# Modulation rounds with a ring and fixed steps of their own beside the blocks of w2, half by half on TensorE or on VectorE, and w2 loaded two blocks to a buffer

## The chip, the cores and the metric

The kernel runs on one core of a Trainium2 chip. The metric is the device time of one execution in microseconds (us). The engines named below are TensorE (PE, with its weight loads as PEld), VectorE (DVE), ScalarE (ACT), GpSimd (POOL) and SyncE (SP), which issues the loads.

## What is computed

A trunk of two layers over 256 latent tokens and 256 context tokens of width 1024. Each layer is a feed-forward half-step, a mixer (even: spatial gating and attention; odd: mLSTM) and a second feed-forward half-step. Every half-step and mixer takes its shift, scale and gate from the modulation, nine vectors of 1024 for each layer, once for the latent and once for the context tokens. All is float32.

```python
def modulate(z, g, shift, scale):
    return rmsnorm(z, g) * (1 + scale) + shift

def swiglu(z, w13, w2):
    gate, up = jnp.split(z @ w13, 2, axis=-1)
    return (jax.nn.silu(gate) * up) @ w2

s_lat = jax.nn.silu(c)
s_ctx = jax.nn.silu(c_ctx)[None, :]
for l in range(DEPTH):
    m_l = (s_lat @ mod_w[l] + mod_b[l]).reshape(b, N_MOD, 1, d)
    m_c = (s_ctx @ mod_w[l] + mod_b[l]).reshape(1, N_MOD, 1, d)
    h = h + 0.5 * m_l[:, 2] * swiglu(modulate(h, norm_g[l, 0], m_l[:, 0], m_l[:, 1]), ffn_w13[l, 0], ffn_w2[l, 0])
    ...
    h = h + m_l[:, 5] * y_l
    h = h + 0.5 * m_l[:, 8] * swiglu(modulate(h, norm_g[l, 2], m_l[:, 6], m_l[:, 7]), ffn_w13[l, 1], ffn_w2[l, 1])
    ...
```

## The kernel before

**Products.** A float32 weight is split into two parts of reduced float32, `whi` (ScalarE's cast, in `wsplit`) and `wlo` (VectorE's subtraction of that from the raw weight), and activations likewise; each product is three matmuls, high by high, high by low and low by high (`mm3`, L116 to L118). The split weights lie in a ring of four (`NWH`), so splits run up to four blocks ahead of PE. Raw weights lie in a ring of four buffers of 1 MB, `rawp`.

**Stages.** In time: a start; the first ffn of layer 0 to 410.7 us; the even mixer to 550; the second ffn of layer 0 to 968.6; the first ffn of layer 1 to 1346.5; the odd mixer to about 1545; the last ffn, latent tokens only. The first three are `ffn512`, both sets of tokens together, 512 columns. It cuts the hidden width of 22 tiles of 128 into two chunks, 12 and 10 (`CHUNKS`). For a chunk it first makes the hidden columns, pair by pair, from w13 (seven products of 24 matmuls of 256 columns for a pair, L791), then multiplies them by w2: four blocks of output columns (`dp`, two PSUM banks each), each over the chunk's tiles in blocks of up to four (three blocks in the first chunk; 4, 4 and 2 in the second). A whole block is 24 matmuls of 512 columns. A block of w2 is 512 KB and takes a whole buffer of `rawp`. In the second chunk the last `dp` is done in two halves of 256 columns, and the next norm's sums stand beside it. After a `dp`, `finish` adds the result to the residual with the gate. The gate of a half-step is itself modulation, needed in the first chunk: there the first `dp`'s `finish` is kept back in `late` until after the first block of the second `dp`, the fourth in all.

**Modulation.** The 9 x 1024 columns of `mod_w` of a layer are 18 rounds of 512 columns; a round's weights are two loads of 1 MB, its halves. Four rounds are done at the start in another form. The others:

- On VectorE (`mod_round_dve`, 24 rounds): eight tiles of 128 rows, for each set of tokens one multiply-add over 128 x 512 (L265 the first, L267 the rest), 16 operations, or 8 where only latent tokens need the round (from `LATROUND`). Four small matmuls then add VectorE's 128 partial sums into a PSUM bank (`mod_ps`, L277). When a group of rounds (`GROUPS`) is full, it is copied out, transposed and written to `modT`.
- On PE (`mod_direct`, 8 rounds in pairs): 16 matmuls a pair, which the trace records as 32, of 32 stationary columns into one bank (`mdir_ps`, L311); then `direct_columns`: a copy on ScalarE (L324), four transposes (`mdirT_ps`) and two small operations on VectorE. One pair stands in the first ffn and one in the third, between the first and the second `dp` of the first chunk; two pairs in the even mixer.

**Order.** Engines run their instructions in program order, as a scheduler lays it out from the order of the code and from priorities. `tick` calls `fill` after each block of w2; `FILL` gives 2.6 steps of VectorE rounds per block in the first chunk and 2.2 in the second, each raised by `LEAD`; the small matmuls are raised by `GROUPED`. All rounds take their loads from `rawp`, by `wraw` (L99), in the one SyncE queue that also issues w2 (L961). The odd mixer's `run` calls `fill` too, but in the profile no round is left for it.

Of the kernel before, what the change touches and what calls it, by code (L numbers as in the profile page):

```python
# [26 lines left out]
LEAD = 60  # L27
GROUPED = 400
FILL = ((2.6, 2.2), (2.6, 2.2), (2.6, 2.2))
GROUPS = (((6, 12), (16, 18)), ((0, 4), (6, 10), (10, 12), (12, 16), (16, 18)))  # L30
LATROUND = (1, 10)
MIXDIRECT = {4: (12, 13), 8: (14, 15)}
SOFF = 2
FILLODD = range(13, 25)
# [12 lines left out]
def tile_trunk(  # L47
# [132 lines left out]
    s_st = const.tile([P, KD, SOFF + 32], F32, name="s_st")  # L180
    dve.memset(s_st, 0.0)
# [39 lines left out]
    def mod_round(k, raw):  # L221

        ps = abank("mod_ps")
        for i in range(4):
            for j in range(4):
# [3 lines left out]
                    s_st[:, kh * 4 + i, SOFF:],  # L229
# [18 lines left out]
    filler = []  # L248
    group = {}
    current = [None]  # L250
    turn = [None]
    hidp = [None]
    until = [(1, 17)]

    def mod_round_dve(l, r, hp):

        nv = 1 if (l, r) >= LATROUND else 2
        acc = hp.tile([P, nv, 512], F32, tag="mod_acc", name="mod_acc", bufs=1)
        for kh in range(2):
            raw = wraw(mod_w[l], 4 * kh, 4, r * 512, 512)  # L260
            for k in range(4):
                for v in range(nv):
                    s1 = s_st[:, 4 * kh + k, SOFF + v : SOFF + v + 1]
                    if kh == 0 and k == 0:
                        dve.tensor_scalar(acc[:, v], raw[:, k], s1, None, op0=ALU.mult)  # L265
                    else:
                        dve.scalar_tensor_tensor(acc[:, v], raw[:, k], s1, acc[:, v], op0=ALU.mult, op1=ALU.add)  # L267
                    if nv == 2 and v == 1 or nv == 1 and k % 2 == 1:
                        yield
        r0, n = next((a, b - a) for a, b in GROUPS[l] if a <= r < b)  # L270
        m = r - r0
# [3 lines left out]
        with tc.high_priority(offset=GROUPED):  # L275
            for j in range(4):
                pe.matmul(  # L277
                    ps[32 * j : 32 * (j + 1), : nv * P],
                    onehot[:, MAXG - 1 - m : MAXG + 31 - m],
                    acc[:, :, j * P : (j + 1) * P],  # L280
                    start=(m == 0),
                    stop=(m == n - 1),
                    tile_position=(0, 32 * j),
                )
        if m < n - 1:
            return

        sb = tmp.tile([P, T], F32, tag="sil", name="mod_sb2", bufs=NSIL)
        act.copy(sb[:, : nv * P], ps[:, : nv * P])
        pt = abank("modT_ps")  # L290
# [3 lines left out]
        for v in range(nv):  # L294
# [5 lines left out]
            )  # L300

    def mod_direct(l, rounds):
# [3 lines left out]
        for m, r in enumerate(rounds):  # L306
            raws = [wraw(mod_w[l], 4 * kh, 4, r * 512, 512) for kh in range(2)]
            for i in range(2):
                for j in range(4):
                    k = 2 * j + i  # L310
                    pe.matmul(  # L311
                        ps[32 * j : 32 * (j + 1), :],
                        s_st[:, k, SOFF - 2 * m : SOFF + 32 - 2 * m],
                        raws[k // 4][:, k % 4],
                        start=(m == 0 and i == 0),
                        stop=(m == n - 1 and i == 1),
                        tile_position=(0, 32 * j),
                    )
        return lambda: direct_columns(l, rounds, ps)

    def direct_columns(l, rounds, ps):
        n = len(rounds)
        sb = tmp.tile([P, T], F32, tag="sil", name="mdir_sb", bufs=NSIL)
        act.copy(sb, ps)  # L324
        pt = abank("mdirT_ps")
        for b in range(4):
            tr(pt[:, b * P : (b + 1) * P], sb[:, b * P : (b + 1) * P])
        red = tmp.tile([P, 4, 4], F32, tag="mod_red", name="mod_red", bufs=1)
        dve.tensor_reduce(
            red, pt.rearrange("p (b j c) -> p b c j", b=4, j=4)[:, :, :4], axis=AX.X, op=ALU.add  # L330
# [7 lines left out]
        )  # L338

    def fill(n=1, more=True):  # L340

        for _ in range(n):
            while True:
                if current[0] is None:
                    if not filler or filler[0] > until[0]:
                        return
# [11 lines left out]
    def mvec(l, v):  # L358
# [3 lines left out]
        while current[0] is not None or filler:  # L362
            nxt_round = turn[0] if current[0] is not None else filler[0]
            if nxt_round > (l, end):
                break
# [1587 lines left out]
```

## Time and profile before

| | us |
|---|---|
| median of three runs (1728.83 to 1732.63) | 1730.41 |
| profiled execution, its own time | 1736.36 |
| its span in the trace | 1734.6 |
| PE busy in the span | 1677.1 (97%) |
| DVE busy | 1328.6 (77%) |
| ACT busy | 769.8 (44%) |

The profile is of one execution, so its durations add up against 1736.36, not against the median. Busy time of PE counts overlapping matmuls once; a 512-column matmul is recorded with 0.39 us but the next starts 0.23 us later, so starts, not durations, give PE's pace. The granted clock is a share of 2.4 GHz; over the span it is 0.985.

### The profile page before, as it was taken

Reading aid. Unit: us, or ns where it says so; the run is one execution under the profiler, and the core shown is the slowest. Engines: PE = TensorE matmul, PEld = TensorE weight load, DVE = VectorE, ACT = ScalarE, POOL = GpSimd, SP = SyncE. Lnnn points to the kernel's source line nnn. Section 1 sums busy time; section 2 is a strip of 40 time slices with the busy share of each in tenths; the row PEclk is TensorE's granted clock in tenths of the full one; section 3 lists DMA queues with packets and bytes.
Section 4 is the critical chain, followed back from the end, with each engine's and each line's share of the span. In section 5 each row is a group of like instructions: output and inputs, shape, how many; then the busy total and the mean of one; then the engine's idle time right before and its main releaser. Section 6 shows DMA issues by size and latency. Waiting matters only on the chain.

```text
span 1734.6 us, 29987 instructions
## 1 busy us (share of the span) xinstructions
PE 1677.1 (97%) x12310; PEld 1520.0 (88%) x12310; DVE 1328.6 (77%) x2138; ACT 769.8 (44%) x1217; POOL 89.6 (5%) x109
## 2 busy tenths in 40 slices
PE   7999899999999999989999999999999999999998
PEld 5799589978977999968997999769998799899998
DVE  5897688876765699998888898689886955695554
ACT  4454125523665465412552555214542654364443
POOL 0000000002442000000000000000000001100000
PEclk8999999999999999999999999999999999999999
DMA  9445543253235033465325333575256432136552
GB/s 277 139 137 186 201 158 122 93 177 119 84 136 146 29 119 102 154 213 164 120 83 184 96 128 110 210 264 169 86 195 185 133 111 73 50 128 213 189 179 71
DMA packets 227868, 248.54 MB, mean 143 GB/s; under 512 B 10648, under 2 KB 193940, under 8 KB 227732
## 3 DMA queue, kind: packets, MB, share of 16 engines
q1 hardware_dynamic: 227700, 246.63, 44.6%
q8 instruction: 96, 1.57, 0.4%
q14 instruction: 40, 0.33, 0.1%
q10 hardware_dynamic: 32, 0.01, 0.0%
HBM read 245.56 MB, written 1.05 MB: 142 GB/s over the span
## 4 chain that ended last, share of the span: by engine, by line
PE 55%; issue 12%; DVE 9%; DMA 2%; ACT 1%; POOL 1%; DVEq 0%; SPq 0%; POOLq 0%; ACTq 0%
PE pb L791 11%; PE ps L118 8%; PE ps L116 8%; PE ps L117 8%; PE pc L791 5%; PE pa L791 2%; DVE mod_acc L267 2%; DVE wlo L111 2%; PE ps L1045 2%; PE ps L1046 2%; PE ps L1047 2%; DMA raw<-in_mod_w_dram 1%; PE nd_ps L1744 1%; PE nd_ps L1741 1%; PE sc_ps L1336 1%
## 5 line engine op out<-in xcount | busy, mean ns | idle before, releaser
L110 ACT CAST whi<-raw 128x1024 fp32r<-128x1024 f32 (+2 forms) x204 | 206.9, 1017 | 369.5 <-PE ps L117 169.4
L111 DVE TENSOR_TENSOR wlo<-raw,whi 128x1024 fp32r<-128x1024 f32 (+2 forms) x204 | 239.6, 1181 | 108.4 <-ACT whi L110 108.0
L116 PE MATMUL ps<-hh,whi 128*128 128x512 f32 (+1 forms) x764 | 273.4, 358 | 10.1 <-ACT whi L110 10.1
L118 PE MATMUL ps<-hh,wlo 128*128 128x512 f32 (+1 forms) x764 | 271.3, 356 | 3.2 <-DVE wlo L111 3.2
L117 PE MATMUL ps<-hl,whi 128*128 128x512 f32 (+1 forms) x764 | 271.3, 355 | 0.0
L116 PE MATMUL ps<-zhi,whi 128*128 128x256 f32 (+2 forms) x688 | 209.1, 307 | 3.5 <-ACT zhi L416 1.8
L118 PE MATMUL ps<-zhi,wlo 128*128 128x256 f32 (+2 forms) x688 | 207.6, 305 | 1.8 <-DVE wlo L111 1.7
L117 PE MATMUL ps<-zlo,whi 128*128 128x256 f32 (+2 forms) x688 | 208.0, 304 | 0.0
L267 DVE SCALAR_TENSOR_TENSOR mod_acc<-raw,s_st,mod_acc 128x512 f32<-128x512 f32 x280 | 196.3, 746 | 11.1 <-DMA raw<-in_mod_w_dram 10.0
L110 ACT CAST whi<-rpl 128x1024 fp32r<-128x1024 f32 x116 | 121.7, 1052 | 149.1 <-DMA rpl<-in_ffn_w_dram 41.1
L116 PEld LDWEIGHTS ps<-hh,whi 128*128 128x128 f32 x764 | 145.9, 191 | 34.6 <-ACT whi L110 11.4
L118 PEld LDWEIGHTS ps<-hh,wlo 128*128 128x128 f32 x764 | 146.1, 191 | 30.0 <-DVE wlo L111 4.8
L117 PEld LDWEIGHTS ps<-hl,whi 128*128 128x128 f32 x764 | 145.9, 191 | 22.2 <-issue 1.2
L111 DVE TENSOR_TENSOR wlo<-rpl,whi 128x1024 fp32r<-128x1024 f32 x116 | 140.7, 1220 | 15.2 <-ACT whi L110 14.9
L116 PEld LDWEIGHTS ps<-zhi,whi 128*128 128x128 f32 x688 | 131.2, 191 | 11.5 <-ACT zhi L416 2.3
L118 PEld LDWEIGHTS ps<-zhi,wlo 128*128 128x128 f32 x688 | 130.9, 191 | 7.7 <-DVE wlo L111 2.4
L117 PEld LDWEIGHTS ps<-zlo,whi 128*128 128x128 f32 x688 | 131.3, 191 | 4.8 <-issue 0.4
L791 PE MATMUL pc<-zhi,wlo 128*128 128x256 f32 x440 | 124.1, 282 | 0.0
L791 PE MATMUL pc<-zlo,whi 128*128 128x256 f32 x440 | 123.9, 282 | 0.0
L791 PE MATMUL pc<-zhi,whi 128*128 128x256 f32 x440 | 123.8, 281 | 0.0
L791 PEld LDWEIGHTS pc<-zhi,wlo 128*128 128x128 f32 x440 | 83.2, 189 | 0.0
L791 PEld LDWEIGHTS pc<-zhi,whi 128*128 128x128 f32 x440 | 83.2, 189 | 0.0
(383 smaller groups left out, 4223.6 us busy)
## 6 DMA issues: line engine op xcount, KB each, us to landing
raw<-in_mod_w_dram SPq DMA_DIRECT2D x64, 1024.0 KB
raw<-in_ffn_w_dram SPq DMA_DIRECT2D x62, 512.0 KB
raw<-in_ffn_w_dram SPq DMA_DIRECT2D x30, 1024.0 KB
rpl<-in_ffn_w_dram SPq DMA_DIRECT2D x58, 512.0 KB
rsum<-in_ffn_w_dram SPq DMA_DIRECT2D x29, 512.0 KB
ra<-in_ffn_w_dram SPq DMA_DIRECT2D x29, 512.0 KB
raw<-in_ml_w_in_dram SPq DMA_DIRECT2D x12, 1024.0 KB
mod<-in_mod_w_dram SPq DMA_DIRECT2D x16, 512.0 KB
```

What stands on the lines that cost most here:

```text
L110: act.copy(hi, view)
L111: dve.tensor_tensor(lo, view, hi.bitcast(F32), op=ALU.subtract)
L116: pe.matmul(ps, ah, bh, start=start, stop=False)
L117: pe.matmul(ps, ah, bl, start=False, stop=False)
L118: pe.matmul(ps, al, bh, start=False, stop=stop)
L267: dve.scalar_tensor_tensor(acc[:, v], raw[:, k], s1, acc[:, v], op0=ALU.mult, op1=ALU.add)
L791: pe.matmul(o, a[:, k, cs], b[:, k], start=fresh and j == 0 and k == 0 and n == 0, stop=j == 1 and k == 3 and n == 2, skip_group_check=True,)
L1045: pe.matmul(o, zh, wh[:, k % 4], start=(k == 0), stop=False)
L1046: pe.matmul(o, zh, wl[:, k % 4], start=False, stop=False)
L1047: pe.matmul(o, zl, wh[:, k % 4], start=False, stop=(k == KD - 1))
L1336: pe.matmul(sc[:, :nk], qst[t][:, p, w], kst[:, w, part, key0 * P : key0 * P + nk], start=(part == 0), stop=(part == 1),)
L1741: pe.matmul(nd3[:, d, :], wts[h][:, d * HT + t * P : d * HT + (t + 1) * P], vs[p][:, t, w, :], start=True, stop=False)
```

## The change

1. *A ring for modulation.* Inside `ffn512`, loads of modulation go to a ring `q` of two buffers of 1 MB (shared with one w13 block and two saved products of a pair), by `mod_load`. In the mixers they stay in `rawp`, with a priority of their own (`RAWLEAD`); the last ffn has one buffer for them. The stationary columns lie closer together for it (`s_flat`).
2. *Two blocks of w2 to a buffer*: `load_block` hands out halves of a 1 MB buffer.
3. *Fixed steps.* `STEPS` names, for each block of w2 in order, what is put behind it: D is the next step of `mod_direct`, which is half a round on PE (four instructions, eight records), or the transposes; V is one tile of a VectorE round, two operations, or the end of a round. `FILL`, `fill` and `tick` go, and so does the priority.
4. *Who does which round.* `DIRECT` gives each `ffn512` a pair and a single round on PE, `ONDVE` three rounds on VectorE. The even mixer gets a third pair (`MIXDIRECT`); the odd mixer gets one pair and four VectorE rounds (12 to 15, latent tokens only); the last ffn gets rounds 16 and 17 on VectorE. In all 17 rounds are on PE and 15 on VectorE.
5. *The gate* and the kept `finish` come once the round is there (`made`): after the fifth block instead of the fourth.
6. *Small matmuls* of a VectorE round: one set of four for each set of tokens, half as wide (L298), without priority in `ffn512`.

```diff
-FILL = ((2.6, 2.2), (2.6, 2.2), (2.6, 2.2))
...
+DIRECT = (((0, (4, 5)), (0, (9,))), ((0, (16, 17)), (1, (3,))), ((1, (4, 5)), (1, (9,))))
+ONDVE = (((0, 6), (0, 7), (0, 8)), ((1, 0), (1, 1), (1, 2)), ((1, 6), (1, 7), (1, 8)))
+STEPS = (
+    ("D", "D", "D", "DV", "DVV", "VV", "VV", "V", "VVV", "VV", "VV", "VV", "V"),
+    ("V", "V", "V", "VV", "V", "VD", "V", "VD", "VD"),
+)
-MIXDIRECT = {4: (12, 13), 8: (14, 15)}
+MIXDIRECT = {1: (10, 11), 4: (12, 13), 7: (14, 15)}
+ODDDIRECT = (10, 14, 18)
...
-FILLODD = range(13, 25)
+FILLODD = range(9, 33)
...
+    def mod_load(l, r, kh):
+
+        if mraw[0] is None:
+            with tc.high_priority(offset=RAWLEAD):
+                return wraw(mod_w[l], 4 * kh, 4, r * 512, 512)
+        raw = mraw[0]().rearrange("p (k c) -> p k c", c=512)
+        nc.sync.dma_start(
...
-    def mod_direct(l, rounds):
+    def mod_direct(l, rounds, halves=1):
 
         n = len(rounds)
         ps = abank("mdir_ps")
         for m, r in enumerate(rounds):
-            raws = [wraw(mod_w[l], 4 * kh, 4, r * 512, 512) for kh in range(2)]
-            for i in range(2):
+            for kh in range(2):
+                raw = mod_load(l, r, kh)
                 for j in range(4):
...
+                if (halves == 2 or kh == 1) and (m < n - 1 or kh == 0):
+                    yield
         sb = tmp.tile([P, T], F32, tag="sil", name="mdir_sb", bufs=NSIL)
         act.copy(sb, ps)
+        yield
...
+            mraw[0] = lambda: hp.tile([P, 2048], F32, tag="q", name="mraw", bufs=2)
...
                     def load_block(k0, n):
-                        r = rawp.tile([P, 2048], F32, tag="raw", name="raw2", bufs=4)[:, : n * 256]
-                        v = r.rearrange("p (k c) -> p k c", c=256)
+                        if not spare:
+                            t = rawp.tile([P, 2048], F32, tag="raw", name="raw2", bufs=4)
+                            spare.extend([half_tile(t, 1), half_tile(t, 0)])
+                        v = spare.pop()[:, :n]
...
-                            if ch == 0 and dp == 1 and k0 == 0:
-                                if len(late) > 1:
-                                    late.pop(0)()
+                            if half == 0:
+                                advance(next(todo, ""))
+                            if late and made(l, 2 + 6 * i):
                                 dve.tensor_scalar(gate, mvec(l, 2 + 6 * i), 0.5, None, op0=ALU.mult)
-                                late.pop(0)()
-                            if not last:
-                                tick(rates[ch] * n / 4)
...
+        work = (s for r in range(12, 16) for s in mod_round_dve(l, r))
+        direct = mod_direct(l, (10, 11))
...
                 if ran[0] in FILLODD:
-                    fill(1)
+                    with tc.high_priority(offset=LEAD):
+                        next(work, None)
+                if ran[0] in ODDDIRECT:
+                    next(direct, None)
```

PE in the w2 stage of the first ffn, first chunk, before: the end of the third block, the whole pair (16 instructions) with its transposes and one set of sums, then the fourth block.

```order
962 L117 MATMUL ps<-hl,whi 128x512
963 L118 MATMUL ps<-hh,wlo 128x512
964 L311 MATMUL mdir_ps<-raw,s_st 32x512 x16
965 L121 MATMUL mdirT_ps<-ident,mdir_sb 128x128
966 L277 MATMUL mod_ps<-mod_acc,onehot 32x256 x4
967 L121 MATMUL mdirT_ps<-ident,mdir_sb 128x128 x3
968 L116 MATMUL ps<-hh,whi 128x512
969 L117 MATMUL ps<-hl,whi 128x512
```

PE in the same stage after the change: the end of the first block, one half-round (four instructions, from the ring's buffer `mraw`), the start of the second block. The same row stands behind the second, third and fourth block, 25 rows apart.

```order
939 L125 MATMUL ps<-hl,whi 128x512
940 L126 MATMUL ps<-hh,wlo 128x512
941 L336 MATMUL mdir_ps<-mraw,s_st 32x512 x4
942 L124 MATMUL ps<-hh,whi 128x512
943 L125 MATMUL ps<-hl,whi 128x512
```

The pair has come apart into four pieces, the first of them two blocks earlier, and its transposes no longer follow it at once.

SyncE's loads around the same stage before: modulation (L99) and w2 (L961) take turns in the one ring, and each w2 row is one block.

```order
53 L961 DMA raw_1833<-in_ffn_w_dram 128x4x256
54 L99 DMA raw<-in_mod_w_dram 128x4x512 x4
55 L961 DMA raw_1894<-in_ffn_w_dram 128x4x256
56 L99 DMA raw<-in_mod_w_dram 128x4x512
57 L961 DMA raw_1953<-in_ffn_w_dram 128x4x256
58 L99 DMA raw<-in_mod_w_dram 128x4x512
59 L961 DMA raw_1991<-in_ffn_w_dram 128x4x256
60 L961 DMA raw_2031<-in_ffn_w_dram 128x4x256
```

SyncE's loads there after the change: w2 blocks 3 to 10 (L971) stand together, with one modulation load (L269) between, and the other loads of the pair's halves follow the w13 sum `rsum`.

```order
47 L971 DMA raw_1822<-in_ffn_w_dram 128x4x256 x2
48 L971 DMA raw_1903<-in_ffn_w_dram 128x4x256
49 L269 DMA mraw<-in_mod_w_dram 128x4x512
50 L971 DMA raw_1903<-in_ffn_w_dram 128x4x256
51 L971 DMA raw_1991<-in_ffn_w_dram 128x4x256 x2
52 L971 DMA raw_2056<-in_ffn_w_dram 128x4x256 x2
53 L772 DMA rsum<-in_ffn_w_dram 128x4x256
54 L269 DMA mraw<-in_mod_w_dram 128x4x512 x3
```

Modulation's loads have moved behind w2's, and four of them no longer stand in one piece ahead of a block.

VectorE in the odd mixer, in the chain of scans that makes the gates, before:

```order
1296 L1540 SCALAR_TENSOR_TENSOR M<-LI,mst 64x128
1297 L1545 TENSOR_TENSOR mst<-bcum,M 64x1
1298 L1540 SCALAR_TENSOR_TENSOR M<-LI,mst 64x128
1299 L1545 TENSOR_TENSOR mst<-bcum,M 64x1
1300 L1540 SCALAR_TENSOR_TENSOR M<-LI,mst 64x128
1301 L111 TENSOR_TENSOR wlo<-raw,whi 128x1024
1302 L1545 TENSOR_TENSOR mst<-bcum,M 64x1
```

The same chain after the change:

```order
1198 L287 TENSOR_SCALAR mod_acc<-raw,s_st 128x512
1199 L1551 SCALAR_TENSOR_TENSOR M<-LI,mst 64x128
1200 L289 SCALAR_TENSOR_TENSOR mod_acc<-raw,s_st,mod_acc 128x512
1201 L1556 TENSOR_TENSOR mst<-bcum,M 64x1
1202 L119 TENSOR_TENSOR wlo<-raw,whi 128x1024
1203 L1551 SCALAR_TENSOR_TENSOR M<-LI,mst 64x128
1204 L289 SCALAR_TENSOR_TENSOR mod_acc<-raw,s_st,mod_acc 128x512
1205 L1556 TENSOR_TENSOR mst<-bcum,M 64x1
1206 L289 SCALAR_TENSOR_TENSOR mod_acc<-raw,s_st,mod_acc 128x512
```

Four modulation operations stand between the scans now, and further on one more split stands among the copies ahead of the convolution.

## Rows read from the trace of the kernel before

**Rows 1.** The page's busy times: us, share of the span, instructions.

```profile
PE 1677.1 (97%) x12310; PEld 1520.0 (88%) x12310; DVE 1328.6 (77%) x2138; ACT 769.8 (44%) x1217; POOL 89.6 (5%) x109
```

**Rows 2.** Windows, w2 and odd mixer: length, busy PE PEld DVE ACT POOL, clock, DMA, GB/s.

```profile
161.30:245.00 83.70, 77.10 (x352) 57.19 (x351) 59.58 (x90) 14.73 (x16) 0.00 (x0) 0.96 0.59 202
...
346.90:410.70 63.80, 61.09 (x333) 50.76 (x333) 42.02 (x72) 17.37 (x25) 0.70 (x1) 0.97 0.48 156
...
728.80:809.00 80.20, 73.42 (x334) 56.26 (x333) 73.52 (x112) 14.34 (x17) 0.00 (x0) 0.96 0.58 195
908.40:968.60 60.20, 60.20 (x342) 49.86 (x341) 47.79 (x82) 17.49 (x25) 0.70 (x1) 1.00 0.46 154
1098.30:1184.60 86.30, 80.19 (x371) 58.64 (x370) 60.05 (x92) 14.83 (x17) 0.00 (x0) 0.94 0.72 244
1286.70:1346.50 59.80, 59.73 (x344) 49.81 (x341) 42.70 (x73) 16.82 (x26) 1.65 (x2) 1.00 0.69 215
1346.50:1545.00 198.50, 195.00 (x1403) 175.31 (x1403) 139.41 (x368) 101.11 (x201) 19.27 (x26) 0.98 0.30 95
```

**Rows 3.** The same windows, modulation's operations (L267) alone: length, VectorE busy, clock, DMA.

```profile
728.80:809.00 80.20, 43.48 (x64) 0.96 0.58 195
```

**Rows 4.** PE's waits in the three first-chunk stretches: us, times, longest.

```profile
PE ps L116 <- ACT whi L110: 5.5, 2, 4.7
...
PE mod_ps L277 <- DVE mod_acc L267: 3.9, 2, 3.2
PE ps L118 <- DVE wlo L111: 2.9, 1, 2.9
...
PE ps L116 <- ACT whi L110: 4.6, 2, 3.0
```

**Rows 5.** Waits of ScalarE and of SyncE's queue, 161.3 to 245.

```profile
ACT whi L110 <- DMA raw<-in_ffn_w_dram: 28.3, 8, 8.2
...
SPq L961 <- PE mdir_ps L311: 11.5, 2, 10.8
```

**Rows 6.** Timeline of PE, third ffn: start, us, operation; the pair, its transposes.

```profile
1116.84 3.64 PE L311 MATMUL mdir_ps<-raw,s_st 128*32 128x512 f32 x32
1121.21 0.66 PE L121 MATMUL mdirT_ps<-ident,mdir_sb 128*128 128x128 f32 x4 [0.73 <-ACT mdir_sb L324]
```

**Rows 7.** Timeline of PE around one group of modulation sums beside w2.

```profile
218.18 0.39 PE L116 MATMUL ps<-hh,whi 128*128 128x512 f32 x1
218.41 0.40 PE L117 MATMUL ps<-hl,whi 128*128 128x512 f32 x1
218.73 0.64 PE L277 MATMUL mod_ps<-mod_acc,onehot 128*32 128x256 f32 x8
219.30 0.50 PE L118 MATMUL ps<-hh,wlo 128*128 128x512 f32 x1
219.64 0.39 PE L116 MATMUL ps<-hh,whi 128*128 128x512 f32 x1
```

**Rows 8.** Timeline of PE around such a group between products of w13.

```profile
301.52 0.28 PE L791 MATMUL pb<-T4h,whi 128*128 128x256 f32 x1
301.73 0.62 PE L277 MATMUL mod_ps<-mod_acc,onehot 128*32 128x256 f32 x2
...
304.88 0.39 PE L791 MATMUL pb<-T4l,whi 128*128 128x256 f32 x1
```

**Rows 9.** Timelines of SyncE's queue and VectorE: a load of 1 MB and its user.

```profile
345.48 0.37 SPq L99 DMA_DIRECT2D raw<-in_mod_w_dram  x1
...
349.37 0.75 DVE L267 SCALAR_TENSOR_TENSOR mod_acc<-raw,s_st,mod_acc 128x512 f32<-128x512 f32 x1 [3.31 <-DMA raw<-in_mod_w_dram]
```

**Rows 10.** Timeline of VectorE: two splits.

```profile
198.54 2.35 DVE L111 TENSOR_TENSOR wlo<-raw,whi 128x1024 fp32r<-128x1024 f32 x2
```

**Rows 11.** Timelines of VectorE and PE in the odd mixer, around the convolution.

```profile
1389.97 0.75 DVE L1444 SCALAR_TENSOR_TENSOR cy<-ps,cols,cy 128x510 f32<-128x510 f32 x1
...
1391.86 0.39 PE L118 MATMUL ps<-zhi,wlo 128*128 128x512 f32 x1
1392.37 0.36 PE L1045 MATMUL ps<-whi,zhi 128*128 128x256 f32 x1
```

More of the change, by code (lines that the diff above doesn't have):

```diff
@@ L1 @@
[L1 removed]
+from contextlib import ExitStack, nullcontext
 import concourse.bass as bass
@@ L274, in mod_round_dve @@
         ps = group["ps"]
[L275 to L284, printed above, removed]
+        with tc.high_priority(offset=GROUPED) if mraw[0] is None else nullcontext():
+            for v in range(nv):
+                for j in range(4):
+                    pe.matmul(
+                        ps[32 * j : 32 * (j + 1), v * P : (v + 1) * P],
+                        onehot[:, MAXG - 1 - m : MAXG + 31 - m],
+                        acc[v][:, j * P : (j + 1) * P],
+                        start=(m == 0 and v == 0),
+                        stop=(m == n - 1 and v == nv - 1),
+                        tile_position=(0, 32 * j),
+                        skip_group_check=True,
+                    )
         if m < n - 1:
+            yield
             return
@@ L300, in mod_round_dve @@
             )
-    def mod_direct(l, rounds):
+        ready.update((l, i) for i in range(r0, r0 + n))
+    def mod_direct(l, rounds, halves=1):
         n = len(rounds)
@@ L338, in direct_columns, with made @@
         )
[L340 to L346, printed above, removed]
-                    turn[0] = filler.pop(0)
-                    current[0] = mod_round_dve(*turn[0], hidp[0])
-                with tc.high_priority(offset=LEAD):
-                    done = next(current[0], "end") == "end"
-                if done:
-                    current[0] = None
-                    if n == 1 and not more:
-                        return
-                    continue
-                break
-    def mvec(l, v):
-        end = next((b for a, b in GROUPS[l] if a <= 2 * v + 1 < b), 0) - 1
-        if end < 0:
-            return modT[l][:, v * 8 : (v + 1) * 8, :]
[L362 to L365, printed above, removed]
-            fill(1)
+        ready.update((l, r) for r in rounds)
+        yield
+    ready = {(0, r) for r in range(4)}
+    def made(l, v):
+        return {(l, 2 * v), (l, 2 * v + 1)} <= ready
+    def mvec(l, v):
+        assert made(l, v), (l, v)
         return modT[l][:, v * 8 : (v + 1) * 8, :]
@@ L668, in ffn @@
                                 )
-                        if not last:
-                            tick(fill2)
-                        elif half == 0 and k0 == 0:
-                            while current[0] is not None or (until[0] == (0, 11) and filler and filler[0] <= until[0]):
-                                fill(1, more=False)
                     for j in range(2):
@@ L1412, in wout @@
             return v
-        og_ = None
+        mraw[0] = None
+        og_ = rounds = None
         for n in range(16):
             if n in MIXDIRECT:
-                columns_of = mod_direct(0, MIXDIRECT[n])
-            elif n - 1 in MIXDIRECT:
-                columns_of()
+                rounds = mod_direct(0, MIXDIRECT[n])
+            if rounds is not None:
+                next(rounds, None)
             if n + 2 < 16:
@@ L1881, in tile_trunk @@
     HALVES = [(0, HT), (HT, T)]
-    filler.extend([(0, r) for r in range(6, 12)] + [(0, 16), (0, 17)] + [(1, r) for r in range(18) if r not in (4, 5)])
     nxt = Next(0, 1)
-    until[0] = (0, 11)
-    ffn512(0, 0, z, nxt, FILL[0], first=first, direct=(4, 5))
+    ffn512(0, 0, z, nxt, DIRECT[0], ONDVE[0], first=first)
     z = nxt.z
```

126 lines of the change are left out of this document (64 added, 62 removed).

## The prediction

> **What bounds the kernel now.** The page first: TensorE is busy 97% of the span [rows 1]. That is an average, so the next view is the busy time of the engines by stage, over the six stretches in which PE multiplies by w2 [rows 2]. The three stretches of the first hidden chunk take 83.7, 80.2 and 86.3 us. Their own work is 4 column blocks x 3 blocks of w2 x 24 matmuls of 512 columns, 288 in all, which start 0.23 us apart (218.18 and 218.41 in [rows 7]; over the run 0.2325): 67.0 us bare. So 16.7, 13.2 and 19.3 us a stage go elsewhere, 49.2 us together. The three stretches of the second chunk take 63.8, 60.2 and 59.8 us against 56.0 bare (180 matmuls at 0.2325 and 120 half as wide): little is left there.
>
> Where the 49 us go is in the list of waits, PE's own. In the first and the third stretch PE waits 5.5 and 4.6 us for the ScalarE half of a weight split; in the second 3.9 us for VectorE's modulation sums and 2.9 us for the VectorE half of a split [rows 4]. ScalarE in turn waits 28.3 us for w2 to land, and SyncE, which issues those loads, waits for the modulation's matmuls before it can issue w2 (11.5 us) [rows 5]: modulation and w2 share one ring of four buffers. VectorE is busy 73.5 of 80.2 us in the second of these stretches, 43.5 of them in 64 modulation steps [rows 2, 3]. So these stages are bound by VectorE's modulation and by w2 coming late behind it, not by w2's matmuls. After the waits PE's clock is at 1.2 GHz for a while: the granted clock is 0.96, 0.96 and 0.94 there, against 1.00 in the second chunk of the middle layer [rows 2], a loss of 3.3, 3.2 and 5.2 us (0.04 or 0.06 of the stretch).
>
> **What the change takes and gives in the first chunk.** (1) *VectorE.* Per ffn512, first chunk, the fixed steps put 16 k-steps of two operations on it, 32 operations at 0.68 us (43.48/64 in [rows 3]) = 22 us, instead of 32 to 44 us. The first stretch's 59.6 us [rows 2] becomes about 59.6 - 33 + 22 = 49 of some 73: no longer the bound. (2) *Loads.* w2 no longer stands behind modulation: eight blocks of it fit in the four buffers, and modulation has two buffers of its own. (3) *On PE.* Four half-rounds of a pair, each alone behind a block. The old pair was four half-rounds in one piece: 32 records in 3.64 us [rows 6], 0.91 each; entering costs 0.09 (218.41 to 218.73 is 0.32, not 0.23), leaving about 0.10 (219.30 to 219.64 is 0.34), both read where the smaller kind of group stands [rows 7], less an overlap of some 0.1 at the end of the record: 1.0 each, 4.0 together. Their transposes: 0.66 [rows 6], less the overlap, 0.5, without the 0.73 us wait ahead of them, since ScalarE's copy now has a whole block of 5.6 us. Two groups that pass VectorE's sums into PSUM: the old one moves the next matmuls by 219.64 - 218.41 - 2 x 0.2325 = 0.77 us [rows 7]; now eight instructions of half the columns instead of four, taken as 0.8: 1.6. With 0.4 for the stage's start: 67.0 + 4.0 + 0.5 + 1.6 + 0.4 = **73.5 us** a stage, 220.5 for three against 250.2: **-29.7**. The clock's share of 11.7 us is in that, since no stall is left that pulls it down.
>
> The Trainium skill, TensorEngine Tiling (Array Packing), section Key Properties, says that a change of the tiling mode drains the TensorE; that speaks against cutting a pair into four pieces. The rows price it: 0.09 in and 0.10 out [rows 7], so three cuts more cost 0.6 us a stage, and the sum has them.
>
> What comes next there? *The half-round's load.* A 1 MB load issued at 345.48 is used at 349.37 [rows 9], 3.9 us, with no other megabyte ahead. From the order of SyncE I place the second half-round's load at some 4 us into the stage and its use at 5.6 + 1.0 + 5.6 = 12.2: 8 us for a load of 4 to 7. The third is issued when the first is done, at 6.6, and due at 18.8. Covered; if the cover is gone, each microsecond late is a microsecond of PE. *The gate.* It now follows the fifth block, not the fourth, since the transposes stand there: 5 x 5.6 + 4.5 = 32.5, plus VectorE's chain through reduction, gate and eight residual additions with some modulation steps among them, about 4: 36.5. The third column block needs those PSUM banks at 6 x 5.6 + 4.5 = 38. Slack 1.5 us; I allow a residue of **+2** for all such stalls (0 to +8, three stages of up to 2.7, the size of the waits in [rows 4]).
>
> **Second chunk.** The clean stretch of 60.2 us [rows 2] holds three sum groups (3 x 0.77) and their transposes (0.4): 57.5 without. After: two half-rounds 2.0, transposes 0.5, one group 0.8, its transposes 0.3: 61.1 each, 183.3 against 183.8: **-0.5** (-3 to +4).
>
> **Groups that stood between w13's products.** In the first ffn the group at 301 to 305 came in four pieces among narrow products: from 301.52 to 304.88 are 3.36 us with four products of 0.117 in it [rows 8], 2.9 lost. A second one like it costs 2.1 (at 1241, half the columns) and one at the end of a stage 1.1 (at 1286, with its wait). The fixed order has none there: **-6.1** (-6.1 to -4).
>
> **Given back in the mixers.** *Even:* one more pair on PE, 3.64 + 0.5 + edges [rows 6]: **+5** (4.3 to 7, the upper end if the extra pair waits once as in [rows 4]). *Odd:* this stretch had no modulation and PE is busy 195.0 of its 198.5 us [rows 2], so nothing hides. A pair 3.64 + 0.2 + 0.5 = 4.4; four groups at 0.45 to 0.55, 2.0, with transposes 2.3. VectorE gets 32 operations, four of them and one split (1.18, half of the pair in [rows 10]) inside the gates' chain that ends in the convolution at 1389.97: 0.4 + 3 x 0.68 + 1.18 = 3.6 us later. PE already waited 0.28 us for that (1391.86 to 1392.37, less the pitch, [rows 11]); the pair put before it gives some 1.5 back: +2.3. Modulation's loads and PSUM banks there are the shared ones, as in [rows 5]: +2. **+11** (6.5, with chain and sharing covered, to 14). *Last ffn:* two rounds' groups, **+1**.
>
> **Sum.** -29.7 - 0.5 - 6.1 + 2 + 5 + 11 + 1 = -17.3, from the profiled execution's own 1736.36 us to 1719. That execution is 5.95 above the runs' median of 1730.41; the same difference from the median gives **1713 us**. A measurement of this kernel tells 0.2% (3.5 us) from no change, so faster is below 1727 and slower above 1734.
>
> **Rivals.** *A, slower: half-rounds wait for their loads.* SyncE issues in program order, so a load that waits for its buffer holds those behind it, and a half-round cannot be passed by the next w2 matmul on PE. It decides from a landing more than 8 us after issue; at, say, 10.5 us each of 18 half-rounds is 2.5 us late: +45, -17 + 45 = +28, 1758. For it: 28.3 us of waits on landing [rows 5], and 244 GB/s with clock 0.94 in the third stretch [rows 2]. Against: the 3.9 us of [rows 9], and what a stage loads (6 MB of w2, 8 of modulation, 2 to 3 of w13 in 73.5 us, some 230 GB/s) has been moved before at 244.
>
> *B, the mixers take more.* Of the odd mixer's 32 operations more land inside chains that PE waits for, or the shared ring holds up the projection: odd +18, even +8 instead of 11 and 5: 1723. For it: those stretches have 3.5 us of idle PE [rows 2]. Against: VectorE is only 70% busy there (139.4 of 198.5).
>
> *C, PE is the bound throughout.* The change moves nine rounds onto PE: 9 x 2 x 1.0 = 18 us more, six more sets of transposes 3, nine fewer sum groups -5: +16. If the gaps of the first chunk are PE's own, nothing comes off: 1746. Against: the waits named in [rows 4, 5], and 77.1 busy of 83.7 at a lower clock [rows 2]. The Trainium skill, Perfetto Trace Analysis, section Identifying the Most-Contended Engine, would have the busiest engine relieved first, and that is PE by [rows 1], with the caution that matmul occupancy measures it badly; this change loads PE further. By that rule the answer is C; the stage view speaks against it.
>
> *D, it doesn't do what it says:* VectorE and loads go on setting the first chunk's pace, since the residual and split chains are what is late (gate 1.5 us of slack). Then half of the 29.7 comes: -17 + 15 = -2, 1728.
>
> **Numbers.** Forecast with its own range of 1700 to 1720: 0.64; B 0.16; A 0.07; C 0.06; D 0.07. The low end is all costs at their low bounds, -29.7 - 3 - 6.1 + 0 + 4.3 + 6.5 + 1 = -27, 1703, and a little below for a clock that stays up elsewhere. The high end takes in B and half of D: 1729. Left out: A, C, half of D, and 0.02 below. Faster 0.80 (forecast, B), same 0.07 (D), slower 0.13 (A, C).
>
> **What would show it.** Right: the first chunk's stretches at 72 to 76 us with the clock at 1.00 and VectorE near 49 us; the half-rounds without a wait for a DMA; the sum groups gone from w13; the odd mixer 9 to 13 us longer. Wrong: PE waits on mraw (A); odd mixer over 215 us (B); first chunk still above 79 with waits on whi, wlo or the residual's banks (D); above 79 without waits (C).

## The result

The changed kernel takes 1715.40 us (median of four runs, 1713.99 to 1718.17) against 1731.52 for the kernel before in the same comparison (median of four, 1728.83 to 1734.17). The ratio is 0.9909, with a 95% interval of 0.9888 to 0.9930: faster by 16.1 us. The profiled execution took 1718.17, with a span of 1716.5 us, 18.1 below the span of before.

The page of the changed kernel, busy times (us, share of the span, instructions), beside [rows 1]:

```profile
PE 1680.2 (98%) x12475; PEld 1521.7 (89%) x12475; DVE 1253.0 (73%) x2019; ACT 774.3 (45%) x1221; POOL 90.8 (5%) x109
```

PE is busy 3 us longer than before and idle 21 us less (36.3 against 57.5): what went is waiting. The rounds that moved to PE lengthen its busy time so little partly because less of it passes at the lower clock: the granted clock over the span is 0.993 instead of 0.985. The same windows as in [rows 2], of the changed kernel (length, busy PE, PEld, DVE, ACT, POOL, clock, DMA share, GB/s): the three first-chunk w2 stretches, the second-chunk one of the first ffn, the odd mixer up to the last ffn's first matmul, and the last ffn.

```profile
158.20:231.50 73.30, 73.30 (x346) 54.99 (x345) 50.00 (x72) 14.38 (x16) 0.00 (x0) 1.00 0.53 179
...
331.20:392.50 61.30, 61.30 (x354) 50.86 (x353) 36.16 (x65) 18.81 (x27) 0.70 (x1) 1.00 0.46 150
...
714.60:788.00 73.40, 73.40 (x346) 55.09 (x348) 50.12 (x73) 14.46 (x16) 0.00 (x0) 1.00 0.53 178
...
1079.00:1152.30 73.30, 73.30 (x346) 55.00 (x348) 49.99 (x72) 14.43 (x16) 0.00 (x0) 1.00 0.54 179
...
1313.20:1513.60 200.40, 193.64 (x1402) 169.74 (x1401) 154.41 (x390) 97.69 (x197) 19.17 (x25) 0.98 0.46 152
1513.60:1710.50 196.90, 194.17 (x1639) 192.57 (x1637) 125.42 (x184) 88.44 (x131) 1.28 (x2) 0.99 0.54 177
```

In the first chunk PE is busy from end to end at the full clock, and the three stretches, once 80 to 86 us, are alike to 0.1 us. The last two windows in the kernel before, cut at the same matmuls, were:

```profile
1346.50:1536.50 190.00, 186.50 (x1332) 166.81 (x1332) 132.22 (x354) 96.94 (x195) 18.57 (x25) 0.98 0.29 94
1536.50:1728.70 192.20, 191.45 (x1622) 190.54 (x1620) 114.87 (x166) 88.06 (x130) 1.35 (x2) 1.00 0.49 159
```

From the start of each stage's first matmul to that of the next stage's, all in us:

| stage | predicted | measured |
|---|---|---|
| w2, first chunk, three | -29.7 | -28.2 |
| w2, second chunk, three | -0.5 | -0.1 |
| w13 of the second chunk, three | -6.1 | -6.3 |
| residue of stalls in w2 | +2 | 0 (in the first row) |
| even mixer | +5 | +3.9 |
| odd mixer | +11 | +10.4 |
| last ffn | +1 | +4.7 |
| start, before the first ffn | 0 | -2.9 |
| first chunk's w13 and the rest | 0 | +0.4 |
| sum | -17.3 | -18.1 |

(The first row runs to the first matmul of the next w13, and so has in it the 0.5 us group of sums that stands behind the last block; to the last w2 matmul it is 220.0 against 250.2.)

### The profile page after: what moved, and what is told of

Same layout as the page of the kernel before. It is cut to its first block, busy times and chain, and to the rows that moved or that the text cites. A ratio compares the mean times of both kernels' runs of the same rounds, so it can differ in the third digit from the quotient of the medians.

```text
span 1716.5 us, 30178 instructions
## 1 busy us (share of the span) xinstructions
PE 1680.2 (98%) x12475; PEld 1521.7 (89%) x12475; DVE 1253.0 (73%) x2019; ACT 774.3 (45%) x1221; POOL 90.8 (5%) x109
## 5 line engine op out<-in xcount | busy, mean ns | idle before, releaser
L126 PE MATMUL ps<-hh,wlo 128*128 128x512 f32 (+1 forms) x764 | 267.6, 350 | 0.0
L125 PE MATMUL ps<-hl,whi 128*128 128x512 f32 (+1 forms) x764 | 267.5, 350 | 0.0
L289 DVE SCALAR_TENSOR_TENSOR mod_acc<-mraw,s_st,mod_acc 128x512 f32<-128x512 f32 x140 | 99.3, 748 | 11.9 <-DMA mraw<-in_mod_w_dram 11.2
L1051 PE MATMUL ps<-whi,zhi 128*128 128x256 f32 x288 | 83.6, 291 | 3.5 <-DVE cy L1458 3.0
```

The source lines that it names most:

```text
L125: pe.matmul(ps, ah, bl, start=False, stop=False)
L126: pe.matmul(ps, al, bh, start=False, stop=stop)
L289: dve.scalar_tensor_tensor(acc[v], raw[:, k], s1, acc[v], op0=ALU.mult, op1=ALU.add)
L1051: pe.matmul(o, zh, wh[:, k % 4], start=(k == 0), stop=False)
```

## The experiments

Times by stage are from each one's trace, by the same marks as above; the start of the program differs from trace to trace by up to 3 us, so stages are compared, not totals, unless rounds are given.

### What held the first chunk up before: loads, operations or pace

**The loads of VectorE's rounds left out of the kernel before.**

```diff
-            raw = wraw(mod_w[l], 4 * kh, 4, r * 512, 512)
+            raw = still[:, 0:4].unsqueeze(2).to_broadcast([P, 4, 512])
```

> The kernel before, with the loads of VectorE's modulation rounds left out (their operations stay, on a small resident tile, so these columns of the modulation are not computed; the rounds on PE keep their loads). Theory (VectorE's time and the shared ring both cost): the middle first-chunk w2 stretch, in which VectorE was busy 73.5 of 80.2 us, stays at 77 to 80; the first and third, where PE waited for splits behind late w2 loads, fall from 83.7 and 86.3 to about 76. Rival (the late loads alone): all three fall to 71 to 73. Second rival (VectorE alone): none falls by more than 2.

The three stretches went from 83.7, 80.2 and 86.3 to 80.8, 71.2 and 76.5. The middle one, in which VectorE stayed busiest, fell to the bare matmuls and sums:

```profile
720.60:791.80 71.20, 70.69 (x326) 54.77 (x325) 68.85 (x102) 14.15 (x15) 0.00 (x0) 1.00 0.29 92
```

VectorE is busy 68.9 of 71.2 us here and PE waits 0.5. So a VectorE at 97% does not hold PE up by itself: the theory failed for the middle stretch, where it had said 77 to 80. VectorE has less to do in it than before, though: 61 operations of modulation instead of 74, and 4.7 us less of busy time. The theory failed for the first stretch too, which took 80.8 where it had said 76: VectorE stood idle for its one accumulator, which PE's sums give back, and PE waited for a residual:

```profile
DVE mod_acc L268 <- PE mod_ps L280: 19.9, 3, 18.7
...
PE ps L116 <- DVE hT L457: 1.9, 1, 1.9
```

**The loads kept, three of four operations on each left out.**

```diff
-                    if kh == 0 and k == 0:
+                    if k > 0:
+                        pass
+                    elif kh == 0 and k == 0:
```

> The kernel before, with the loads of all rounds kept but only one tile of four multiplied of each load on VectorE, so these columns of the modulation are not computed. Theory: the middle first-chunk stretch falls from 80.2 to about 73, the first and third stay above 78, since w2 still lands behind modulation in the one ring. Rival (loads alone): all three stay within 2 us. Second rival (VectorE alone): all three fall to 72 to 75.

77.3, 72.0 and 77.2. The middle stretch falls as far as without the loads. The theory failed for the first and third, which do not stay above 78; of their 77, 67.0 are w2, some 7 the pair on PE with its transposes and the sums.

**One pace changed, loads and ring as before.**

```diff
-FILL = ((2.6, 2.2), (2.6, 2.2), (2.6, 2.2))
+FILL = ((2.6, 2.2), (2.0, 2.2), (2.6, 2.2))
```

> The kernel before with one number changed: in the second ffn, first chunk, VectorE's rounds are paced at 2.0 steps a block instead of 2.6 (some 14 of 64 operations move to later stages), loads and ring as before. Theory (the pace of VectorE's rounds holds buffers, w2 stands behind them): the middle first-chunk stretch falls from 80.2 to 72 to 75. Rival (the shared ring alone): it stays within 2 us of 80.2.

The middle stretch fell from 80.2 to 74.6, the other two stayed at 82.8 and 85.1, as they should. The number of VectorE operations in it went only from 64 to 56 records (L267 alone), and ScalarE still waited 30.4 us for w2 to land:

```profile
725.10:799.70 74.60, 71.39 (x325) 54.63 (x325) 69.52 (x104) 14.16 (x15) 0.00 (x0) 1.00 0.60 199
```

```profile
ACT whi L110 <- DMA raw<-in_ffn_w_dram: 30.4, 7, 10.1
...
PE mod_ps L277 <- DVE mod_acc L267: 2.3, 3, 1.2
PE ps L118 <- DVE wlo L111: 0.9, 2, 0.5
```

The 5.6 us that went are just what these operations lost in time (43.5 to 37.9 us), and what PE still waits for is VectorE. By itself this run fits a stretch bound by VectorE as well as one held up by late loads.

The three together speak for a coupling rather than an engine alone. A modulation load takes a buffer of the ring, VectorE gives it back when its operations are through, and w2's load stands behind it in SyncE's order. Take away the loads, or the operations, or slow the pace a little, and most of the splits come early enough again. This is argued and not shown: all three runs also left VectorE less to do in the middle stretch (61, 18 and 64 operations instead of 74), and none parts the one from the other.

### Which part of the change does it

**Modulation back in the raw ring.**

```diff
-            mraw[0] = lambda: hp.tile([P, 2048], F32, tag="q", name="mraw", bufs=2)
+            mraw[0] = lambda: rawp.tile([P, 2048], F32, tag="raw", name="mraw", bufs=4)
```

> The changed kernel with modulation's loads back in the ring of the raw weights (four buffers) inside the ffn stages, all else as changed. Theory: the ring of its own matters; first-chunk stretches go from 73.3 to 76 to 79 us with PE waiting for splits behind w2 loads. Rival: with fewer rounds on VectorE and the fixed steps the ring is not needed; 73 to 74.

73.3, 73.3 and 73.3 us: the theory failed, the rival held.

**One block of w2 to a buffer.**

```diff
-                            spare.extend([half_tile(t, 1), half_tile(t, 0)])
+                            spare.append(half_tile(t, 0))
```

> The changed kernel with one block of w2 to a buffer again (four blocks ahead instead of eight), modulation in its own ring. Theory: no difference in the w2 stretches (73.3 and 61.2, each within 0.5), because a block of 512 KB lands in about 3 us and is needed every 5.6 to 6.8. Rival: the longer prefetch carries it; first-chunk stretches 76 or more.

Again 73.3 three times, as the theory said.

**Both undone.** The two edits above together.

> The changed kernel with both load parts undone together: modulation in the ring of the raw weights inside the ffn stages, and one block of w2 to a buffer. Each alone left the first-chunk stretches at 73.3 us. Theory now: what the change gains there comes from the fixed steps with fewer rounds on VectorE, and the loads follow; 73.3 to 74. Rival: either cover is enough and one of the two is needed; without both w2 is late again, 76 to 80, with PE waiting for splits.

And again, here with the first stretch and ScalarE's longest waits in it:

```profile
157.90:231.20 73.30, 73.30 (x346) 55.02 (x348) 50.66 (x72) 13.98 (x15) 0.00 (x0) 1.00 0.58 193
```

```profile
ACT whi L118 <- PE ps L125: 27.8, 7, 5.3
ACT whi L118 <- DMA raw<-in_ffn_w_dram: 20.7, 5, 11.9
```

ScalarE waits 20.7 us for w2 here, much as in [rows 5], and PE for nothing. That wait costs nothing as long as the splits keep a block ahead of PE. So neither load part of the change, alone or together with the other, is worth anything measurable in these stretches. What is left is the fixed steps: 16 tiles of VectorE rounds where before there were 26 to 37 (32 operations against 52 to 74), in other places and without the priority, and PE's pair in pieces. Which of these counts most, no run tells. The change also gives VectorE's rounds accumulators in turn where before had one; no run takes that back, but VectorE's wait for the one was 0.9 us in the middle stretch before, and not among its waits in the other two.

**The fixed steps raised by the old priority, on top of both undone.**

```diff
             for s in steps:
-                next(work[s], None)
+                with tc.high_priority(offset=LEAD):
+                    next(work[s], None)
```

> The changed kernel with both load parts undone (as in the run where that left the first chunk at 73.3 us) and every fixed step of modulation in the ffn stages raised by the priority that VectorE's rounds had before. What is then left of the change there is the number of rounds on VectorE and their place. Theory: the amount counts, not the priority; 73.3 to 74.5, with VectorE near 50 us. Rival: raised steps again stand ahead of splits and of w2's loads; 76 to 80.

84.1 us a stretch and 1772.1 in all: neither theory's number, and not by the rival's way either. PE waits for no data, and VectorE has 48.8 us to do. The window, and PE's timeline in it:

```profile
162.80:246.90 84.10, 84.10 (x346) 57.14 (x343) 48.83 (x69) 13.72 (x15) 0.00 (x0) 1.00 0.46 153
```

```profile
167.09 0.39 PE L124 MATMUL ps<-hh,whi 128*128 128x512 f32 x1
167.41 1.05 PE L336 MATMUL mdir_ps<-mraw,s_st 128*32 128x512 f32 x2
168.39 0.49 PE L125 MATMUL ps<-hl,whi 128*128 128x512 f32 x1
168.81 1.05 PE L336 MATMUL mdir_ps<-mraw,s_st 128*32 128x512 f32 x2
169.79 0.49 PE L126 MATMUL ps<-hh,wlo 128*128 128x512 f32 x1
```

The priority raised PE's part of the steps as well, and the four instructions of a half-round now stand one by one between matmuls of w2. Each costs 1.40 - 0.23 = 1.17 us (168.81 - 167.41, less one w2 matmul), as much as all four in a row. Eight such pieces stand in this stretch, 9.4 us where four half-rounds take 4.8. The sums are strewn in the same way and make up the larger part: 13 pieces at some 0.5 us (211.34 - 210.57, less one w2 matmul) instead of one group of 0.77.

```profile
210.57 0.41 PE L298 MATMUL mod_ps<-mod_acc,onehot 128*32 128x128 f32 x2
210.91 0.50 PE L124 MATMUL ps<-hh,whi 128*128 128x512 f32 x1
211.34 0.41 PE L298 MATMUL mod_ps<-mod_acc,onehot 128*32 128x128 f32 x2
```

It is the effect of [rows 8], where sums stood one by one between w13's products. What the priority does to VectorE's part alone stays open: this run can't tell.

### What a half-round costs, and its cover

**Whole rounds on PE in a step.**

```diff
-            "D": (s for g in direct for s in mod_direct(*g, halves=2)),
+            "D": (s for g in direct for s in mod_direct(*g, halves=1)),
...
-    ("D", "D", "D", "DV", "DVV", "VV", "VV", "V", "VVV", "VV", "VV", "VV", "V"),
-    ("V", "V", "V", "VV", "V", "VD", "V", "VD", "VD"),
+    ("", "D", "", "DV", "DVV", "VV", "VV", "V", "VVV", "VV", "VV", "VV", "V"),
+    ("V", "V", "V", "VV", "V", "V", "V", "VD", "VD"),
```

> The changed kernel with whole rounds on PE in a step instead of half-rounds inside ffn512 (a pair in two pieces instead of four, a single round in one instead of two). The trace of the changed kernel has 1.2 us for a half-round alone, the old pair had 0.91 for each of four together. Theory: each piece fewer saves 0.25 to 0.3 us, so 73.3 becomes 72.7 to 72.8 and 61.2 becomes 60.9 to 61.0. Rival: a round empties the ring of two at once and the next waits for its loads: 74 or more.

72.7 and 60.9 in all three, 0.3 us for each cut that is gone, and no wait for loads. A half-round in the changed kernel, and a whole round here (PE's timelines):

```profile
163.57 0.40 PE L126 MATMUL ps<-hh,wlo 128*128 128x512 f32 x1
163.89 1.07 PE L336 MATMUL mdir_ps<-mraw,s_st 128*32 128x512 f32 x8
164.89 0.50 PE L124 MATMUL ps<-hh,whi 128*128 128x512 f32 x1
```

```profile
168.78 0.40 PE L126 MATMUL ps<-hh,wlo 128*128 128x512 f32 x1
169.10 1.92 PE L336 MATMUL mdir_ps<-mraw,s_st 128*32 128x512 f32 x16
170.96 0.50 PE L124 MATMUL ps<-hh,whi 128*128 128x512 f32 x1
```

From the w2 matmul ahead to the one behind: 1.32 and 2.18 us. Less one pitch of 0.23 and with 0.1 for the slower start behind it, 1.2 for a half-round alone and 2.05 for two together. One run took 1711.97 us.

**Every modulation load in the ffn stages made twice.** The second goes to the same buffer after the first, so a half-round's weights land later, and SyncE stands still meanwhile.

```diff
-        nc.sync.dma_start(
-            out=raw,
...
+        for _ in range(2):
+            nc.sync.dma_start(
+                out=raw,
...
```

> The changed kernel with every modulation load inside the ffn stages made twice into the same buffer, the second after the first, so each half-round's weights land one transfer (3 to 4 us) later and SyncE stands still meanwhile. Theory: the cover is 3 to 4 us for the second half-round of a pair and more for the others, so the first-chunk stretches go from 73.3 to 73.3 to 76, with at most one wait on a DMA of PE each. Rival A (late loads stop PE at once): about 2.5 us at each of four half-rounds, 80 or more, and 65 or more instead of 61.2 in the second chunk.

75.4, 75.7 and 74.9 us in the first chunk, 61.3 unchanged in the second. PE's only waits in the first stretch, and SyncE's longest there:

```profile
PE mdir_ps L337 <- DMA mraw<-in_mod_w_dram: 2.0, 2, 1.7
...
SPq L270 <- DMA mraw<-in_mod_w_dram: 28.4, 10, 4.5
```

SyncE stood still for 28.4 us, up to 4.5 at a time, and PE lost 2.0. But the edit moved more than the loads: PE's half-rounds stand behind 24, 65, 75 and 113 matmuls of w2 in this run, instead of 24, 48, 72 and 96. So it does not measure the cover that the changed kernel has.

The changed kernel's own trace does, by the semaphore events that it has for each load. In the second `ffn512` the second half-round's load is issued at 718.60 us and has landed at 726.94; PE begins at 727.10 (timelines of SyncE's queue and PE):

```profile
718.60 0.37 SPq L269 DMA_DIRECT2D mraw<-in_mod_w_dram  x1
...
727.10 1.07 PE L336 MATMUL mdir_ps<-mraw,s_st 128*32 128x512 f32 x8
```

The load takes 8.3 us and has 8.5 from its issue to its use, which leaves 0.2 to spare. In the first and third `ffn512` the load takes some 7.5 us and has 1.0 and 0.9 to spare; the other half-rounds of the first chunks have 4.4 us or more. So the loads are covered, but at this one place only just.

### What was given back, and where

**The odd mixer's four VectorE rounds left out**.

```diff
-        work = (s for r in range(12, 16) for s in mod_round_dve(l, r))
+        work = iter(())
```

> The changed kernel without the odd mixer's four VectorE rounds (these columns are left out); its pair on PE stays. Theory: the odd stretch, 200.4 us against 190.0 before, falls to 194 to 195.5: four groups of sums (2.3), the bank wait of 3.0 behind the lengthened gate chain back to 0.3, the rest is the pair. Rival: the pair on PE makes the most of the 10.4; 198 or more.

194.5 instead of 200.4 us: 5.9 for the VectorE rounds, 4.5 above before for the pair on PE. With the rounds, PE's wait for the convolution's bank is this (after, timeline):

```profile
1359.52 0.66 PE L129 MATMUL tokc_ps<-ident,pk 128*128 128x128 f32 x4
1363.19 0.42 PE L1051 MATMUL ps<-whi,zhi 128*128 128x256 f32 x1 [3.02 <-DVE cy L1458]
```

Before it was 0.28 [rows 11]; without the rounds it is not among PE's waits at all. The rounds are not all of its cause, though: in the faster version below, which has none there either, it is 1.5 in a stretch of the same 194.5.

**The last ffn's two VectorE rounds left out**.

```diff
-        work = (s for r in (16, 17) for s in mod_round_dve(l, r))
+        work = iter(())
```

> The changed kernel without the last ffn's two VectorE rounds (left out). In the changed kernel ScalarE's order puts one weight cast behind the activation-table load and three activations at the start of that ffn, and PE waits 2.0 us there and has the lower clock after it; without these rounds the order is as before. Theory: from the last ffn's first matmul to the last matmul 196.9 becomes 191.8 to 192.6, and the 2.0 us wait is gone. Rival: the wait comes from what the odd mixer leaves behind; 195.5 to 196, with the wait.

192.2 us, the time of the kernel before, and the wait is gone:

```profile
1512.40:1704.60 192.20, 191.47 (x1622) 190.57 (x1620) 115.00 (x167) 88.12 (x130) 1.32 (x2) 1.00 0.49 160
```

In the changed kernel, ScalarE's and PE's timelines there were:

```profile
1528.87 1.28 ACT L590 ACT_TABLE_LOAD   x1
1530.17 0.91 ACT L590 ACTIVATE sil<-gu,col 128x256 f32<-128x256 f32 x2
1530.98 0.36 ACT L577 ACTIVATE sil<-ps 128x256 f32<-128x256 f32 x1
1531.24 1.03 ACT L118 CAST whi<-raw 128x1024 fp32r<-128x1024 f32 x1
...
1530.04 0.28 PE L125 MATMUL ps<-zlo,whi 128*128 128x256 f32 x1
1532.33 0.39 PE L124 MATMUL ps<-zhi,whi 128*128 128x256 f32 x1 [2.01 <-ACT whi L118]
```

In the kernel without these rounds, as in the kernel before, casts, `zhi` and `sil` stand in another order around the table load, and PE waits for none of the casts. The two rounds use ScalarE for one copy only. They need not change its order: in the run with doubled loads they are there, ScalarE has the order of the kernel before, and PE does not wait. In two more runs the wait is there, but the clock stays up. Here are the last ffn of the run with doubled loads, and that of the run without the odd mixer's rounds:

```profile
1518.10:1711.70 193.60, 192.70 (x1639) 191.05 (x1637) 124.92 (x185) 88.50 (x131) 1.35 (x2) 1.00 0.61 202
...
1506.60:1702.00 195.40, 192.66 (x1639) 191.03 (x1637) 125.14 (x185) 88.42 (x131) 1.33 (x2) 1.00 0.54 178
```

So of the 4.7 us, 1.4 are the rounds themselves (193.6 less 192.2), 2.0 the wait, and 1.5 the lower clock that follows it in the changed kernel (196.9 less 195.4).

### A faster version

**Whole rounds on PE, and the six late VectorE rounds moved beside w2.** Two of them, latent tokens only, go to each ffn512 as a group of their own, ahead of the three that it has; the odd mixer keeps its pair on PE, the last ffn has none.

```diff
+    ((1, 12), (1, 13), (0, 6), (0, 7), (0, 8)),
+    ((1, 14), (1, 15), (1, 0), (1, 1), (1, 2)),
+    ((1, 16), (1, 17), (1, 6), (1, 7), (1, 8)),
...
+    ("", "D", "", "DV", "DVV", "VV", "VV", "V", "VVV", "VV", "VV", "VV", "VV"),
+    ("VVV", "VV", "VV", "VVV", "VV", "VV", "VV", "VVD", "VD"),
```

> The changed kernel with whole rounds on PE in a step, and with the odd mixer's four and the last ffn's two VectorE rounds moved beside the w2 blocks of the three ffn512 (two each, as groups of two). Theory from the stage prices: first chunk 73.3 (72.7 and one more, smaller sum group), second 61.6, odd stretch 194 to 195, last ffn 192; about 9 us under the changed kernel, 1706 us, ratio 0.985 to the kernel before. Rival: seven more tiles a stage on VectorE in the second chunk make the splits or the next norm late, 63 or more there, and the gain falls to 4 or less.

1706.13 us (median of five, 1704.89 to 1708.17) against 1733.22 for the kernel before on the same chip, ratio 0.9847, interval 0.9833 to 0.9860. This interval lies below that of the changed kernel.

```profile
157.90:231.00 73.10, 73.10 (x347) 55.30 (x349) 49.26 (x72) 14.61 (x17) 0.00 (x0) 1.00 0.60 207
330.70:392.60 61.90, 61.72 (x370) 50.93 (x369) 45.53 (x80) 18.27 (x26) 0.70 (x1) 1.00 0.51 173
...
1312.90:1507.40 194.50, 189.57 (x1367) 166.95 (x1367) 132.30 (x356) 97.41 (x195) 18.64 (x25) 0.99 0.35 113
1507.40:1699.60 192.20, 191.48 (x1622) 190.59 (x1620) 115.01 (x167) 88.22 (x130) 1.31 (x2) 1.00 0.49 160
```

Against the run with whole rounds alone (72.7 and 60.9) the six rounds cost 0.4 us in a first chunk and 0.8 to 1.0 in a second, some 4 us in all; where they had been, 5.9 and 4.7. VectorE had the room: 45.5 of 61.9 us.

## Why the prediction was right, and where its steps were not

The time was right (1713 forecast, 1715.4 measured), and so was its main step: the first chunk's stretches held some 10 us each that could go, a clean stage would take 73.5, and it takes 73.3. The clock is 1.00 in all three (against 0.94 to 0.96 in [rows 2]), VectorE is busy 50 us, the sums are gone from w13, the odd mixer took what was said. That the sum comes so close to the traces (-17.3 and -18.1) is in part luck: 2.9 us saved at the start, which had no term, and 2 of stalls that did not come stand against 3.7 too little put at the last ffn and 1.5 too much gain in the first chunk.

*Loads* failed as a step: the prediction listed the own ring and the deeper prefetch of w2 among what frees PE, and three runs with one, the other and both undone kept 73.3. It gave them no term, so the sum didn't suffer; but "bound by VectorE's modulation and by w2 coming late behind it" was read from a busy share and a list of waits, and the runs show that a VectorE at 97% can stand beside a PE that waits 0.5 us, and a ScalarE that waits 20.7 us for w2 beside a PE that waits for nothing. What holds PE up is in PE's own waits [rows 4]; that they come from the two together is argued above, not shown.

*The half-round* was mis-sized: 1.2 us, not 1.0, 0.8 a stage too little. An overlap was subtracted that isn't there, and the start and end of each piece cost 0.3, not 0.2. The 0.4 for the stage's start, which no row gave, hides part of it: 0.1 is left for it when the pieces are counted at what they took. The sums' price was right (0.77 again, with twice the instructions), but only one of two groups lies inside the 73.3; the other is the 0.5 behind it. The Trainium skill, TensorEngine Tiling (Array Packing), section Key Properties, says that a change of tiling mode drains the TensorE. The traces fit that: a cut costs 0.3 us by the run with whole rounds, 0.6 us a first-chunk stage against this change.

*The gate's bank* and the loads left no stall: the +2 for them was 0. *The even mixer* took 3.9 instead of 5, *the odd* 10.4 instead of 11, split as worked out: 4.5 for the pair (4.4), 5.9 for the VectorE rounds; its bank wait grew by 2.7 (2.3). The +2 for shared loads and banks has no wait of its own in the traces.

*The last ffn* is the term that was wrong, +1 against +4.7. What the rounds add on PE was counted, and by the run with doubled loads it is 1.4; that the scheduler lays out ScalarE's instructions in another order, and that PE waits for it and has the lower clock afterwards, had no term.

*The start* took 2.9 us less in this pair of traces and had no term. In the traces with the start of before the first ffn begins at 28.4 to 30.2 us, in those with the start of after at 25.9 to 28.2. PE waits there for small loads to land and has the lower clock after that. The longest such wait is 2.91 us before and 1.68 after, and the granted clock is 0.50 (1.2 GHz) for 10.2 us before and for 3.4 after (the two windows):

```profile
18.20:28.40 10.20, 8.18 (x46) 4.90 (x43) 6.95 (x23) 4.18 (x12) 0.00 (x0) 0.50 1.05 289
...
21.90:25.30 3.40, 3.03 (x8) 2.01 (x8) 2.87 (x9) 1.31 (x3) 0.00 (x0) 0.50 1.12 355
```

Whether the denser stationary columns or something else in the start does it was not tried.

Of the rivals, A came closer than the prediction had it. Its 3.9 us for a load is misread from [rows 9]: by the semaphore events, VectorE waits at 349.37 for an earlier load, issued at 341.46 and landed at 349.34, and the one issued at 345.48 landed at 353.46. That is 7.9 and 8.0 us (timeline of SyncE's queue):

```profile
341.46 0.37 SPq L99 DMA_DIRECT2D raw<-in_mod_w_dram  x1
```

The prediction gave the second half-round 8 us for a load of 4 to 7; the loads took 7.5 to 8.3 and had 8.5. The cover held there by 0.2 to 1.0 us, which is luck as much as reckoning. For all half-rounds to be late, as A's +45 had it, the others had 4.4 us or more to lose. B and D didn't come. C is answered by the page: PE's busy time rose by 3 us, and the span fell by 18. The Trainium skill, Perfetto Trace Analysis, section Identifying the Most-Contended Engine, says of the engine with the highest occupancy: "Optimize this engine first." Read as a call to give PE less to do, it would have spoken against this change. Here the measurement decides otherwise: PE got nine more rounds and the kernel is faster, since its 97% was an average over stages with and without waits.

## What to carry to other kernels

Read the waits of the engine that ends the stage, not the busy share of those that feed it: a feeder at 97%, or one with 20 us of waits, costs next to nothing while it keeps a block ahead. Where two feeders are coupled through a ring and an in-order queue, easing the pace of one can bring most of the gain (80.2 to 74.6 us here by one number, 73.4 with the whole change), and the separate rings added nothing measurable, so try the number before the structure. A cover read from a trace must be taken from the load that the wait is for. Work moved into a stage must be looked for on every engine of it, in the instruction order, and small matmuls in another tiling mode belong in one piece.

## What the runs showed of the hardware

Four matmuls of 32 stationary columns, each into its own quarter of the array, took no longer than one: a piece of two records cost 1.17 us between w2 matmuls, one of eight 1.20, and one of sixteen 2.05. The price of such work is by the piece and by fours, not by the instruction, which is why instructions of modulation and its sums, strewn among w2's matmuls, made a stretch of 73.3 us one of 84.1. A load of 1 MB took 7.5 to 8.3 us from its issue to its landing for the second half-round of a pair, with another load issued 1.2 us before it, and 4.8 to 5.1 for the fourth, with none issued in the 6 us before.
